# Experts placed by rank: double, full, half and quarter tiles in the two mixture-of-experts stages of a two-layer hybrid block

## The chip, the cores and the metric

The kernel runs on one core of a Trainium2 chip. The metric is the device time of one execution in microseconds (us). Three runs of the kernel before took 1410.01, 1413.93 and 2414.91 us; the median, 1413.93, is the time before.

## What is computed

Two layers act on 256 latent tokens and 256 context tokens of width 1024, all in float32. Layer 0 mixes with a gated delta rule and an S5 scan, layer 1 with latent attention (for the latent tokens alone). Each layer ends in a grouped top-2 mixture of 16 experts, and this is the part that the change touches:

```python
def grouped_moe(h, router_w, router_bias, w_gate, w_up, w_down):
    tok = h.reshape(-1, h.shape[-1])
    scores = jax.nn.sigmoid((tok @ router_w).astype(F32))
    ...
    _, idx = lax.top_k(jnp.where(in_group, choice, -jnp.inf), TOP_K)
    ...
    gates = jnp.sum(jax.nn.one_hot(idx, N_EXPERTS, dtype=F32) * wts[..., None], axis=1)
    out = jnp.zeros(tok.shape, F32)
    for e in range(N_EXPERTS):
        act = jax.nn.silu(tok @ w_gate[e]) * (tok @ w_up[e])
        out = out + gates[:, e:e + 1] * (act @ w_down[e])
```

`in_group` keeps the best of four groups of four experts. Layer 0 sends 512 tokens through its experts, layer 1 only the 256 latent ones, so 1024 and 512 rows in all, two for each token. An expert has a gate and an up matrix of 1024 x 512 and a down matrix of 512 x 1024, 2 MB each, and every layer has its own 16 experts. How many rows an expert gets is known only when the router has run.

## The kernel before

The program is straight-line code for five engines: TensorE (PE in the profile), VectorE (DVE, `V` in the code), ScalarE (ACT, `S`), GpSimd (POOL, `G`) and SyncE (SP), whose queue issues the weight loads. Each engine works off its own instructions one after the other, and waits at one until its operands are ready and its buffers free. The code names the engine of each instruction; the order on each engine is fixed when the kernel is built, by the framework's scheduler. It mostly follows the code, but lets some instructions overtake others (a Silu stands ahead of the result of a down product that the code issues before it), so the order has to be read from the built kernel.

**Placing.** `moe_route` counts the rows of each expert (`num`) and gives every row a tile of 128 rows and a place in it. Rows over an expert's cap go to extra tiles behind the `nst` fixed ones (`ovn`, `ovs`), which `overflow_loop` works off in a loop with as many turns as there are such tiles, up to `NOV`. In layer 0 every expert has one tile (cap 128); the expert with the most rows, if it has over 128, gets two and changes places with expert 8 (`BIGP`), so there are 17 tiles. The numbers of the experts are compile-time constants but for those that may have changed places: their number is read from the table `exi` into a register of SP by `expert_id` (the TENSOR_LOAD of line 1595), and the load's address is worked out from it. In layer 1 the tiles are 8, each with two experts of 64 rows each, in the order of their numbers.

**Weights.** `load_chunk` (line 199) issues the load of half a matrix, 1.05 MB, into one slot of a ring: nine slots in layer 0, 18 in layer 1. An expert is six chunks: gate (`wg`) 0 and 1, up (`wu`) 0 and 1, down (`wd`) 0 and 1.

**Layer 0, `experts0`.** TensorE multiplies here in a rounded float32 format, and gets full precision from three products. `wsplit` makes the high part of a chunk on ScalarE (`hi`, line 1660) and the low part on VectorE (`lo`, line 1661); for the first up chunk alone the low part is made on GpSimd. There are three pairs of such buffers (`HI`). `mm3` multiplies high by high, high by low and low by high: 24 products of 128 x 128 by 128 x 512 for a chunk, 72 for a tile. The rows of a tile come by an indirect DMA on GpSimd (`gather`), are turned on TensorE by `turn` (line 203) in groups of four, and split by `split` (`sp`, lines 1640 and 1641); the gated activations are turned and split in the same way. `gated` is the Silu on ScalarE and a product on VectorE. `write` scales the result of the down matrix on ScalarE (`y`, line 1730) and writes it out by an indirect DMA. The loop over units weaves two experts: gate of unit i, first gate chunk of unit i+1, turning of unit i's activations, second gate chunk of i+1, rows of i+2, down of i, both up chunks of i+1.

**Layer 1, `experts1`.** Products are full float32 here, with no split: each shows as two records on TensorE. Two experts of a tile write the two halves of 64 rows of the same result, so a chunk of each takes part in the same step. The rows of a tile are picked by a product with a one-hot table (`pick`, `sl` on VectorE), the results added back by a product with the gates (`put_back`). The loop weaves in the same way.

Of the kernel before, what the change touches and what calls it, by code (L numbers as in the profile page):

```python
# [31 lines left out]
NOV = 7  # L32
# [4 lines left out]
BIGP = 8  # L37
# [123 lines left out]
def _build(es, tc, I, O):  # L161
# [1136 lines left out]
    def moe_open(l, stack):  # L1298
# [41 lines left out]
        if l == 0:  # L1340
            m.xes = [m.mo.tile([128, D], F32, name=f"xe{i}") for i in range(3)]
            for t in m.xes:
                G.memset(t, 0.0)
            m.io16 = m.mo.tile([128, 16], F32, name="io16")
            m.far = m.mo.tile([128, 16], F32, name="far")
            G.tensor_copy(m.io16, sm[:, SM_IO16:SM_IO16 + 16])
            G.tensor_scalar(m.far[:, 0:BIGP], m.io16[:, 0:BIGP], 16.0 - BIGP, None, op0=OP.add)
            G.tensor_scalar(m.far[:, BIGP:16], m.io16[:, BIGP:16], float(BIGP), None, op0=OP.subtract)
            G.memset(m.far[:, 0:2], -1.0)
        else:  # L1350
            m.h2 = [m.mo.tile([128, D], F32, name=nm("h2k")) for _ in range(2)]
        return m
# [31 lines left out]
    def moe_route(m):  # L1384
        l, n, mo = m.l, m.n, m.mo
        cap = CAP0 if l == 0 else CAP1
        nst = 17 if l == 0 else 8
# [67 lines left out]
        t16, ovn, ovs, dif = rt([128, 16]), rt([128, 16]), rt([128, 16]), rt([128, 16])  # L1455
        if l == 0:


            key, kmx, big, ep = rt([128, 16]), rt([128, 1]), rt([128, 16]), rt([128, 16])
            V.scalar_tensor_tensor(key, num, float(cap), m.far, op0=OP.is_gt, op1=OP.mult)  # L1460
            red(kmx, key, OP.max)
            V.tensor_scalar(big, m.far, kmx, None, op0=OP.is_equal)
            V.tensor_scalar(key[:, 0:1], kmx, 16.0 - BIGP, -16.0, op0=OP.is_ge, op1=OP.mult)
            V.scalar_tensor_tensor(m.io16[:, BIGP:BIGP + 1], kmx, float(BIGP), key[:, 0:1], op0=OP.add, op1=OP.add)
            V.scalar_tensor_tensor(key, m.io16, float(BIGP), big, op0=OP.subtract, op1=OP.mult)
            tt(ep, m.io16, key, OP.subtract)
            m.exi = rt([128, 16], I32, True)
            V.tensor_copy(m.exi, ep)
            first, caps = rt([128, 16]), rt([128, 16])
            V.scalar_tensor_tensor(first, ep, float(BIGP), ep, op0=OP.is_gt, op1=OP.add)  # L1470
            V.tensor_scalar(caps, big, 128.0, 128.0, op0=OP.mult, op1=OP.add)
            V.scalar_tensor_tensor(num, big, -128.0, num, op0=OP.mult, op1=OP.add)
        V.tensor_scalar(ovn, num, float(cap), None, op0=OP.is_gt)
        for j in range(1, 3 if l == 0 else 2):
            V.scalar_tensor_tensor(ovn, num, float(cap + 128 * j), ovn, op0=OP.is_gt, op1=OP.add)
# [4 lines left out]
        if l == 0:  # L1480
            V.tensor_scalar(t16, t16, 128.0, 128.0 * nst, op0=OP.mult, op1=OP.add)
            tt(t16, t16, caps, OP.subtract)
            V.scalar_tensor_tensor(dif, first, 128.0, t16, op0=OP.mult, op1=OP.subtract)
            tt(val, rank, bc(caps[:, None], N16), OP.is_lt)
        else:
            V.tensor_scalar(t16, t16, 128.0, float(128 * nst - cap), op0=OP.mult, op1=OP.add)
            V.scalar_tensor_tensor(dif, sm[:, SM_IO16:SM_IO16 + 16], float(cap), t16, op0=OP.mult, op1=OP.subtract)
            V.tensor_scalar(val, rank, float(cap), None, op0=OP.is_lt)
# [10 lines left out]
        V.scalar_tensor_tensor(rin, tid, -128.0, rin, op0=OP.mult, op1=OP.add)  # L1499

# [83 lines left out]
    def overflow_loop(m, w2, body):  # L1584

        nreg = nc.values_load(m.novi[0:1, 0:1], min_val=0, max_val=NOV,
                              skip_runtime_bounds_check_because="at most 7 tiles can overflow")
# [24 lines left out]
    def experts0(m):  # L1612
        with ExitStack() as st:
# [19 lines left out]
            def split(name, p, n):  # L1633
# [10 lines left out]
                return hi, lo  # L1644

# [54 lines left out]
            def half(u, name, hh, parts=None):  # L1700

                wh, wl = parts or wsplit(gate_up_chunk(0, name, u[0].e, hh), G if (name, hh) == ("wu", 0) else V)
                for j in u:
                    if hh == 0:
                        setattr(j, name, ps(("wg", "wu").index(name)))
# [10 lines left out]
            def down(u):  # L1716
                for nh in range(2):
                    wh, wl = wsplit(down_chunk(0, u[0].e, nh), V)
# [15 lines left out]
            xe, jobs, eids = {}, {}, {0: 0, 1: 1}  # L1734
            order = [[t] for t in range(BIGP)] + [[BIGP, BIGP + 1]] + [[t] for t in range(BIGP + 2, m.nst)]

            def fetch(upto):
                while len(xe) + len(jobs) <= min(upto, m.nst - 1):
                    ti = len(xe) + len(jobs)
                    xe[ti] = gather(m.toki[:, ti:ti + 1])  # L1740

            def job(ti, u):
                if ti not in jobs:
                    if u not in eids:
                        eids[u] = expert_id(m.exi[0:1, u:u + 1])
                    j = jobs[ti] = Job()
                    j.e, j.ti = eids[u], ti
                    j.xT = split("x", turn(xe.pop(ti)), 8)
                return jobs[ti]

            def unit(i):
                return [job(ti, i) for ti in order[i]]
# [438 lines left out]
```

## Time and profile before

| | us |
|---|---|
| median of three runs | 1413.93 |
| the profiled execution | 1414.94 |
| its span in the profile | 1412.7 |
| first layer up to its experts (0 to 605) | 605 |
| first layer's experts (605 to 941.3) | 336.3 |
| second layer up to its experts (941.3 to 1155) | 213.7 |
| second layer's experts (1155 to 1402.5) | 247.5 |
| the end (1402.5 to 1412.7) | 10.2 |

In the first layer's experts TensorE is busy 322.44 of 336.3 us, VectorE 231.54, ScalarE 233.44, GpSimd 130.21, and the DMA engines move 310 GB/s; in the second layer's TensorE is busy 241.86 of 247.5, VectorE 47.53, ScalarE 20.39, GpSimd not at all, and the DMA engines move 337 GB/s. The clock that TensorE was granted is 0.942 of full speed over the span, 0.98 and 0.99 in the two stages.

A row of a group in the profile gives line, engine, operation and tiles (result <- operands), then busy time, the mean of one in ns, and the idle time of the engine just before them with what ended it. A row of one instruction begins with its start and its duration in us; consecutive alike ones are drawn together with their count. In a stretch of time each engine stands with its busy us and its instructions.

### The profile page before, as it was taken

To read this page: it belongs to the slowest core of one execution; us is meant where nothing else is said; L and a number is where in the kernel's file an instruction comes from. 1 tells how busy PE (TensorE), PEld (TensorE's weight loads), DVE (VectorE), ACT (ScalarE), POOL (GpSimd) and SP (SyncE) were. 2 spreads that over 40 slices of the span, in tenths; PEclk is the share of its full clock that TensorE was granted. 3 is DMA by queue.
4 is the path that set the end of the run, shared out by engine and by line. 5 is a ranking of instruction groups with operands and counts; after the bars stand their busy time and mean duration, and the time that the engine had idled before them with its cause. 6 is when DMAs were issued, how large, how long until landed. Compare 5 with 4: busy or idle time off the path is not lost. (4 is left out here: it accounts for less than half of the span.)

```text
span 1412.7 us, 18172 instructions
## 1 busy us (share of the span) xinstructions
PE 1251.5 (89%) x6716; PEld 847.8 (60%) x6716; DVE 787.6 (56%) x1460; ACT 529.6 (37%) x775; POOL 381.0 (27%) x266
## 2 busy tenths in 40 slices
PE   5889989899788999589999999976999669999996
PEld 1786655555327988457777777744777544444422
DVE  5776756844974465767775577775566151221112
ACT  3312634544112242167776477724365011000100
POOL 1443434320126330334443233353231020000000
PEclk9999999899798999789999999998999779999998
DMA  8713457767488345679999699753034569999980
GB/s 306 257 34 88 155 171 221 225 216 235 149 251 281 131 172 180 273 244 345 377 369 330 227 317 358 283 210 113 32 135 155 194 254 385 398 401 400 399 336 31
DMA packets 201805, 340.40 MB, mean 241 GB/s; under 512 B 31726, under 2 KB 70638, under 8 KB 201201
## 3 DMA queue, kind: packets, MB, share of 16 engines
q1 hardware_dynamic: 171952, 310.97, 62.3%
q10 hardware_dynamic: 23920, 16.95, 3.9%
q0 software_dynamic: 5840, 11.28, 2.2%
q8 instruction: 55, 0.90, 0.3%
q14 instruction: 38, 0.30, 0.1%
HBM read 320.56 MB, written 27.82 MB: 247 GB/s over the span
## 5 line engine op out<-in xcount | busy, mean ns | idle before, releaser
L206 PE MATMUL ps<-hi,sp 128*128 128x512 f32 x816 | 269.5, 404 | 6.0 <-ACT sp L1640 3.7
L1661 DVE TENSOR_TENSOR lo<-ch,hi 128x2048 fp32r<-128x2048 f32 x80 | 185.1, 2330 | 84.6 <-ACT hi L1660 79.8
L1660 ACT ACTIVATE hi<-ch 128x2048 fp32r<-128x2048 f32 x96 | 184.1, 1920 | 80.3 <-PE ps L206 52.8
L206 PEld LDWEIGHTS ps<-hi,sp 128*128 128x128 f32 x816 | 154.0, 190 | 42.7 <-ACT sp L1640 4.4
L206 PE MATMUL ps<-lo,sp 128*128 128x512 f32 x408 | 164.9, 404 | 3.2 <-DVE lo L1661 2.4
L206 PE MATMUL ps<-ch,stat 128*32 128x512 f32 x384 | 93.9, 646 | 31.7 <-DMA ch<-in_ada_w 30.6
L206 PE MATMUL ps<-ch,xT 128*64 128x512 f32 x480 | 119.7, 596 | 0.0
L1661 POOL TENSOR_TENSOR lo<-ch,hi 128x2048 fp32r<-128x2048 f32 x16 | 73.9, 4621 | 160.6 <-ACT hi L1660 160.6
L206 PEld LDWEIGHTS ps<-lo,sp 128*128 128x128 f32 x408 | 77.8, 191 | 26.9 <-DVE lo L1661 8.8
L206 PEld LDWEIGHTS ps<-ch,xT 128*64 128x64 f32 x480 | 36.1, 137 | 66.5 <-issue 65.2
L228 POOL TENSOR_TENSOR frs<-rs,sm 128x1 f32<-128x1 f32 x2 | 1.1, 560 | 259.8 <-DVE rs L227 259.8
L1867 ACT ACTIVATE aT<-ps 128x512 f32<-128x512 f32 x8 | 4.8, 597 | 149.1 <-PE ps L203 149.1
L206 PE MATMUL ps<-ch,aT 128*64 128x512 f32 x240 | 60.0, 596 | 0.7 <-ACTq L1588 0.7
L1880 DVE TENSOR_TENSOR y<-ps,bcm 128x512 f32<-128x512 f32 x16 | 11.1, 691 | 81.8 <-PE ps L206 81.8
L603 POOL TENSOR_TENSOR wl<-raw,wh 128x1024 fp32r<-128x1024 f32 x16 | 38.7, 2417 | 66.2 <-ACT wh L602 66.0
L206 PE MATMUL ps<-hH,wh 128*128 128x512 f32 x128 | 55.0, 430 | 0.0
L206 PEld LDWEIGHTS ps<-ch,stat 128*32 128x32 f32 x384 | 13.6, 112 | 67.7 <-DMA ch<-in_ada_w 35.0
L206 PE MATMUL ps<-hL,wh 128*128 128x512 f32 x128 | 53.8, 420 | 0.0
L206 PE MATMUL ps<-hH,wl 128*128 128x512 f32 x128 | 53.1, 415 | 0.0
L742 DVE SCALAR_TENSOR_TENSOR ac<-ps,convw,ac 128x510 f32<-128x510 f32 (+1 forms) x48 | 35.5, 740 | 23.7 <-ACT ac L738 23.3
L1152 POOL TENSOR_TENSOR ch<-ch,ch 128x512 fp32r<-128x512 f32 (+1 forms) x28 | 31.1, 1127 | 58.3 <-ACT ch L1151 32.3
L206 PE MATMUL ps<-y,sT 128*128 128x512 f32 x80 | 40.9, 642 | 6.4 <-DVE y L1880 2.3
(543 smaller groups left out, 2559.7 us busy)
## 6 DMA issues: line engine op xcount, KB each, us to landing
ch<-in_wg SPq DMA_DIRECT2D x63, 1024.0 KB
ch<-in_wd SPq DMA_DIRECT2D x62, 1024.0 KB
ch<-in_wu SPq DMA_DIRECT2D x61, 1024.0 KB
ch<-in_ada_w SPq DMA_DIRECT2D x88, 512.0 KB
raw<-in_w_in SPq DMA_DIRECT2D x16, 512.0 KB
bcm<-modd ACTq DMA_DIRECT2D x12, 512.0 KB
x<-in_xs SPq DMA_DIRECT2D x8, 512.0 KB
yd<-x SPq DMA_DIRECT2D x8, 512.0 KB
```

Source lines behind the costliest of these rows:

```text
L206: return T.matmul(out, l, r, start=start, stop=stop)
L228: G.tensor_tensor(out, t, bc(neghalf, [128, n]), op=OP.pow)
L603: eng.tensor_tensor(wl, w, wh.bitcast(F32), op=OP.subtract)
L742: V.scalar_tensor_tensor(ac[:, :, lo:hi], pv[:, :, lo + o:hi + o], convw[:, blk, j:j + 1], ac[:, :, lo:hi], op0=OP.mult, op1=OP.add)
L1152: eng.tensor_tensor(lo, src, hi.bitcast(F32), op=OP.subtract)
L1660: last_split[:] = (S.activation(hi, w, AF.Copy), eng.tensor_tensor(lo, w, hi.bitcast(F32), op=OP.subtract))
L1661: eng.tensor_tensor(lo, w, hi.bitcast(F32), op=OP.subtract))
L1867: S.activation(j.aT.rearrange("p k n -> p (k n)"), p, AF.Copy)
L1880: V.tensor_tensor(j.y[:, nh], p, g2[:, nh * 512:(nh + 1) * 512], op=OP.mult)
```

## The change

**Placing.** The router now ranks the experts by their rows. `key` is 16 times the count, with the expert's number taken off to break ties (`tie`); the first `STATIC` experts, 2 in layer 0 and 4 in layer 1, get a constant added, so that they keep the first places whatever their counts. `pos` is an expert's place, and the table `exi` now holds the expert of each place. Places 0 to `STATIC` - 1 are compile-time constants; the others are read into a register when their first chunk is loaded (`experts_of`).

In layer 0, place 2 (the most rows of the others) gets a double tile of 256 rows, places 3 to 9 a full tile of 128 each, and places 0, 1 and 10 to 15 half a tile of 64 each: 13 tiles, 0 (places 0, 1), 1 and 2 (place 2), 3 to 9 and 10 to 12 (places 10 to 15). In layer 1, places 0 to 11 get 64 rows each, two to a tile, and places 12 to 15 get 32 each in one tile: 7 tiles. Rows beyond these go to overflow tiles as before, up to 8 of them.

**Layer 0, half tiles.** A tile with two experts is worked in the form of layer 1: `pair` multiplies the loaded chunks unsplit in full float32, expert by expert in column groups of 64, and `whole` copies the turned rows without a split. Full and double tiles are worked as before. The order of the units is written out: tile 0, tile 10, the double, tile 11, places 3, 4, 5, tile 12, places 6, 7, 8, 9. The first gate chunk's split ahead of the first unit, and the ordering of the first rows behind it, are gone.

**Layer 1.** The order of the tiles is 0, 1, 2, 3, 6 (the quarters), 4, 5.

The diff, cut to what the prediction speaks of:

```diff
-NOV = 7
+NOV = 8
-BIGP = 8
+STATIC = (2, 4)
...
+        V.scalar_tensor_tensor(key, num, 16.0, m.tie, op0=OP.mult, op1=OP.add)
+        tt(cmp, bc(key[:, None, :], SQ), bc(key[:, :, None], SQ), OP.is_gt)
+        red(pos[:, :, None], cmp, OP.add)
         if l == 0:
-            key, kmx, big, ep = rt([128, 16]), rt([128, 1]), rt([128, 16]), rt([128, 16])
...
+            V.tensor_scalar(first, pos, 10.0, 64.0, op0=OP.min, op1=OP.mult)
+            V.scalar_tensor_tensor(first, pos, 2.5, first, op0=OP.is_gt, op1=OP.mult)
+            V.scalar_tensor_tensor(first, pos, 64.0, first, op0=OP.mult, op1=OP.add)
...
+        tt(oh, bc(sm[:, SM_IO16:SM_IO16 + 16, None], SQ), bc(pos[:, None, :], SQ), OP.is_equal)
+        tt(oh, oh, bc(sm[:, None, SM_IO16:SM_IO16 + 16], SQ), OP.mult)
+        red(key[:, :, None], oh, OP.add)
+        m.exi = rt([128, 16], I32, True)
+        V.tensor_copy(m.exi, key)
...
+    def experts_of(m):
+        ids = {p: p for p in range(STATIC[m.l])}
+        def get(p):
+            if p not in ids:
+                ids[p] = expert_id(m.exi[0:1, p:p + 1])
+            return ids[p]
+        return get
...
+            def whole(name, p, n):
+                o = w2.tile([128, n, 128], F32R, tag=f"{name}h", name=nm("wh")).bitcast(F32)
+                for i in range(n // 4):
+                    S.activation(o[:, 4 * i:4 * i + 4], p(i).rearrange("p (k n) -> p k n", k=4), AF.Copy)
+                return o
...
+            def pair(p, xT, k0, ws, n):
+                for q in range(4):
+                    for b, w in enumerate(ws):
+                        c = slice(64 * b, 64 * b + 64)
+                        mm(p[c], xT[:, k0 + q, c], w[:, q, :], k0 + q == 0, k0 + q == n - 1)
...
+                if len(u[0].es) == 2:
+                    pair(getattr(u[0], name), u[0].xT, 4 * hh, [gate_up_chunk(0, name, e(), hh) for e in u[0].es], KD)
+                    return
+                wh, wl = wsplit(gate_up_chunk(0, name, u[0].es[0](), hh), G if (name, hh) == ("wu", 0) else V)
...
-            order = [[t] for t in range(BIGP)] + [[BIGP, BIGP + 1]] + [[t] for t in range(BIGP + 2, m.nst)]
+            one = {p: ([p], [p]) for p in range(3, 10)}
+            order = [([0], [0, 1]), ([10], [10, 11]), ([1, 2], [2]), ([11], [12, 13]), one[3], one[4], one[5],
+                     ([12], [14, 15]), one[6], one[7], one[8], one[9]]
...
-            for i in range(16):
+            for i in range(len(order)):
...
-                    if i < 14 and len(nxt) == 1:
-                        job(order[i + 2][0], i + 2)
+                    if i + 2 < len(order) and len(nxt) == 1:
+                        job(order[i + 2][0][0], order[i + 2][1])
...
-                return job([2 * ti, 2 * ti + 1], lambda kk, i: m.ohT[:, kk, i, c], m.tokf[:, c], m.gate[:, c])
+                return job([lambda p=p: who(p) for p in ((2 * ti, 2 * ti + 1) if ti < 6 else range(12, 16))],
+                           lambda kk, i: m.ohT[:, kk, i, c], m.tokf[:, c], m.gate[:, c])
```

How the change moves instructions is seen in the order of each engine's rows, at three places. The first is ScalarE in layer 0, between two experts with a full tile each. `hi` is the high part of a chunk, `sp` of turned rows or activations, `act` the Silu, `y` the scaled result. Before, `hi_5847` is that of the next expert's first up chunk, whose low part GpSimd makes:

```order
L1660 ACTIVATE hi_5824<-ch_5822 128x2048
L1640 ACTIVATE sp_5755<-ps_5757 128x512
L1660 ACTIVATE hi_5847<-ch_5845 128x2048
L1640 ACTIVATE sp_5785<-ps_5787 128x512
L1713 ACTIVATE act_5882<-ps_5742 128x512
L1640 ACTIVATE sp_5785<-ps_5794 128x512
L1730 ACTIVATE y_5801<-ps_5808,rt_4949 128x512
L1660 ACTIVATE hi_5866<-ch_5864 128x2048
```

After the change the same copy is `hi_5844`:

```order
L1654 ACTIVATE sp_5754<-ps_5756 128x512
L1681 ACTIVATE hi_5820<-ch_5818 128x2048
L1654 ACTIVATE sp_5781<-ps_5783 128x512
L1654 ACTIVATE sp_5781<-ps_5790 128x512
L1745 ACTIVATE act_5878<-ps_5732 128x512
L1681 ACTIVATE hi_5844<-ch_5842 128x2048
L1767 ACTIVATE y_5797<-ps_5804,rt_4949 128x512
```

The high part of the first up chunk has moved from ahead of the turned rows (`sp_5785`, now `sp_5781`) and the Silu to behind them.

The second place is ScalarE after a half-tile pair, where a single expert (place 3) follows; `wh` is the pair's turned activations, `y` its two results, `bcm` a load that ScalarE issues, and `hi_5688` the high part of place 3's first up chunk:

```order
L1664 ACTIVATE wh_5612<-ps_5613 128x512
L1745 ACTIVATE act_5722<-ps_5590 128x512
L1654 ACTIVATE sp_5637<-ps_5639 128x512
L1654 ACTIVATE sp_5637<-ps_5646 128x512
L1211 DMA bcm_5725<-modd 128x1024
L1211 DMA bcm_5727<-modd 128x1024
L1767 ACTIVATE y_5653<-ps_5654,rt_4949 128x512
L1767 ACTIVATE y_5653<-ps_5668,rt_4949 128x512
L1681 ACTIVATE hi_5688<-ch_5686 128x2048
```

On TensorE there the pair's last down product stands directly ahead of the first product that reads `hi_5688`:

```order
L206 MATMUL ps_5668<-ch_5671,wh_5612 64x512
L206 MATMUL ps_5685<-hi_5688,sp_5467 128x512
L206 MATMUL ps_5685<-lo_5689,sp_5467 128x512
```

Such a pair has no counterpart before, where every expert's down matrix was split; what has moved is that a high part now stands behind the results of the down matrix (`y`) and so behind the products that make them.

The third place is the queue of SP in layer 1, behind its first 20 loads. Before it is loads alone; `ISA` below is arithmetic on a register:

```order
L199 DMA x<-in_wu 128x4x512
L199 DMA ch_9654<-in_wu 128x4x512
L199 DMA ch_9680<-in_wg 128x4x512
L199 DMA ch_9682<-in_wg 128x4x512
L199 DMA ch_9699<-in_wg 128x4x512
L199 DMA ch_9701<-in_wg 128x4x512
```

After the change:

```order
L199 DMA x<-in_wu 128x4x512
L199 DMA ch_8915<-in_wu 128x4x512
L1609 TENSOR_LOAD rt_8629
L199 ISA
L199 DMA ch_8944<-in_wg 128x4x512
L1609 TENSOR_LOAD rt_8629
L199 ISA
L199 DMA ch_8949<-in_wg 128x4x512
```

From the third tile on, an expert's number is read from the table before its first load is issued.

More of the change, by code (lines that the diff above doesn't have):

```diff
@@ L1385, in moe_route @@
         l, n, mo = m.l, m.n, m.mo
-        cap = CAP0 if l == 0 else CAP1
-        nst = 17 if l == 0 else 8
+        nst = 13 if l == 0 else 7
         ntl = nst + NOV
@@ L1473, in moe_route @@
-        V.tensor_scalar(ovn, num, float(cap), None, op0=OP.is_gt)
-        for j in range(1, 3 if l == 0 else 2):
-            V.scalar_tensor_tensor(ovn, num, float(cap + 128 * j), ovn, op0=OP.is_gt, op1=OP.add)
+        key, pos, first, caps = (rt([128, 16]) for _ in range(4))
+        cmp, oh = (t[:, i:i + 256].rearrange("p (a b) -> p a b", a=16) for i in (0, 256))
+        SQ = [128, 16, 16]
+        V.scalar_tensor_tensor(key, num, 16.0, m.tie, op0=OP.mult, op1=OP.add)
+        tt(cmp, bc(key[:, None, :], SQ), bc(key[:, :, None], SQ), OP.is_gt)
@@ L1476, in moe_route @@
+        tt(num, num, caps, OP.subtract)
+        V.tensor_scalar(ovn, num, 0.0, None, op0=OP.is_gt)
+        for j in range(1, 4 if l == 0 else 2):
+            V.scalar_tensor_tensor(ovn, num, float(128 * j), ovn, op0=OP.is_gt, op1=OP.add)
         V.tensor_tensor_scan(ovs, ones[:, 0:16], ovn, 0.0, op0=OP.mult, op1=OP.add)
@@ L1479, in moe_route @@
         rank = kp[:, 0:16 * n].rearrange("p (t e) -> p t e", e=16)
[L1480 to L1488, printed above, removed]
+        V.tensor_scalar(t16, t16, 128.0, 128.0 * nst, op0=OP.mult, op1=OP.add)
+        tt(t16, t16, caps, OP.subtract)
+        tt(dif, first, t16, OP.subtract)
+        tt(val, rank, bc(caps[:, None], N16), OP.is_lt)
         tt(val, val, bc(dif[:, None], N16), OP.mult)
@@ L1586, in overflow_loop @@
         nreg = nc.values_load(m.novi[0:1, 0:1], min_val=0, max_val=NOV,
-                              skip_runtime_bounds_check_because="at most 7 tiles can overflow")
+                              skip_runtime_bounds_check_because="at most 8 tiles can overflow")
         with tc.For_i(0, nreg, 1) as it:
@@ L1733, in write, with job @@
                                              out_offset=bass.IndirectOffsetOnAxis(ap=m.rowi[:, cs], axis=0))
[L1734 to L1735 removed]
+            xe, jobs, who = {}, {}, experts_of(m)
+            one = {p: ([p], [p]) for p in range(3, 10)}
+            order = [([0], [0, 1]), ([10], [10, 11]), ([1, 2], [2]), ([11], [12, 13]), one[3], one[4], one[5],
+                     ([12], [14, 15]), one[6], one[7], one[8], one[9]]
+            tiles = [ti for ts, _ in order for ti in ts]
             def fetch(upto):
                 while len(xe) + len(jobs) <= min(upto, m.nst - 1):
[L1739 removed]
+                    ti = tiles[len(xe) + len(jobs)]
                     xe[ti] = gather(m.toki[:, ti:ti + 1])
[L1742 removed]
+            def job(ti, places):
                 if ti not in jobs:
[L1744 to L1745 removed]
                     j = jobs[ti] = Job()
[L1747 to L1748 removed]
+                    j.es, j.ti = [lambda p=p: who(p) for p in places], ti
+                    j.xT = (whole if len(places) == 2 else split)("x", turn(xe.pop(ti)), 8)
                 return jobs[ti]
             def unit(i):
[L1752 to L1753 removed]
+                return [job(ti, order[i][1]) for ti in order[i][0]]
             fetch(1)
[L1755 to L1757 removed]
+            unit(0)
+            unit(1)
             fetch(2)
@@ L1760, in experts0 @@
                 for hh in range(2):
-                    half(unit(0), name, hh, first if (name, hh) == ("wg", 0) else None)
-            for i in range(16):
+                    half(unit(0), name, hh)
+            for i in range(len(order)):
                 cur = unit(i)
@@ L1769, in experts0 @@
                             g2[c] = bc_mod(w1, 0, c, 5, f"g2{c}")
-                fetch(order[i][-1] + 3)
-                nxt = unit(i + 1) if i < 15 else None
+                fetch(tiles.index(order[i][0][-1]) + 3)
+                nxt = unit(i + 1) if i + 1 < len(order) else None
                 if nxt:
@@ L1774, in experts0 @@
                 for j in cur:
-                    j.aT = split("a", turn(j.a), 4)
+                    j.aT = (whole if len(j.es) == 2 else split)("a", turn(j.a), 4)
                 if nxt:
                     half(nxt, "wg", 1)
-                    if i < 14 and len(nxt) == 1:
-                        job(order[i + 2][0], i + 2)
+                    if i + 2 < len(order) and len(nxt) == 1:
+                        job(order[i + 2][0][0], order[i + 2][1])
                     write(cur)
```

65 lines of the change are left out of this document (31 added, 34 removed).

## The prediction

> **What bounds the kernel now.** I read the page first, then stretches of time by engine, then each stage's rows. The profiled execution took 1414.94 us, 1.0 us above the median 1413.93; the sum below is made against 1414.94. Runs of this kernel differ by a few microseconds, so changes within 2% (28 us) count as none.
>
> ```profile
> span 1412.7 us, 18172 instructions
> ...
> 600.00:620.00 20.00, 15.39 (x80) 8.97 (x79) 10.66 (x14) 7.97 (x8) 11.22 (x6) 0.76 0.69 235
> 680.00:700.00 20.00, 19.90 (x91) 15.72 (x90) 15.13 (x10) 15.91 (x13) 8.22 (x4) 1.00 1.04 371
> 1200.00:1220.00 20.00, 20.00 (x100) 9.12 (x98) 4.80 (x10) 2.39 (x4) 0.00 (x0) 1.00 1.05 400
> ```
>
> The columns after the stretch are PE, PEld, DVE, ACT, POOL (busy us, instructions), granted clock, DMA share, GB/s. Both expert stages keep TensorE full and the DMA engines almost so. Which of the two sets the pace has to come from each stage.
>
> First layer, TensorE's rows, from the first transposition to the last weight product:
>
> ```profile
> 604.95 0.65 PE L203 MATMUL ps<-cm,xe 128*128 128x128 f32 x4
> ...
> 907.38 0.63 PE L206 MATMUL ps<-hi,sp 128*128 128x512 f32 x2
> ...
> 911.58 0.63 PE L206 MATMUL ps<-hi,sp 128*128 128x512 f32 x2
> ...
> 914.38 0.40 PE L206 MATMUL ps<-hi,sp 128*128 128x512 f32 x1
> 914.62 0.60 PE L203 MATMUL ps<-cm,act 128*128 128x128 f32 x4
> 914.97 0.48 PE L206 MATMUL ps<-hi,sp 128*128 128x512 f32 x1
> ...
> 940.91 0.40 PE L206 MATMUL ps<-hi,sp 128*128 128x512 f32 x1
> ...
> SPq L199 <- DVE lo L1661: 31.6, 16, 2.6
> 690.56 4.64 POOL L1661 TENSOR_TENSOR lo<-ch,hi 128x2048 fp32r<-128x2048 f32 x1 [10.27 <-ACT hi L1660]
> 709.22 4.61 POOL L1661 TENSOR_TENSOR lo<-ch,hi 128x2048 fp32r<-128x2048 f32 x1 [10.26 <-ACT hi L1660]
> ```
>
> 907.38 to 911.58 holds 18 products, 0.233 us each. A group of four transpositions costs 0.45 with its change-over (0.36 until the next product starts at 914.97, 0.1 in that product). A full tile is 72 products and three groups: 18.15 us. One expert follows the other in 18.66 (690.56 to 709.22), so **the first layer's experts wait for TensorE**. The queue that loads weights waits for buffers to be split (the SPq row, 640 to 700). The stage lasts 604.95 to 941.31 = 336.4 us: 17 tiles are 308.6, waits and slow starts 27.8.
>
> Second layer:
>
> ```profile
> 1155.01 5.73 PE L206 MATMUL ps<-sl,h2k 128*128 128x128 f32 x32 [1.79 <-DVE sl L1824]
> ...
> 1182.49 3.65 PE L206 MATMUL ps<-ch,xT 128*64 128x512 f32 x16
> ...
> 1196.76 3.60 PE L206 MATMUL ps<-ch,xT 128*64 128x512 f32 x16
> ...
> 1225.80 7.04 PE L206 MATMUL ps<-ch,xT 128*64 128x512 f32 x32
> ...
> 1396.10 3.65 PE L206 MATMUL ps<-ch,aT 128*64 128x512 f32 x14
> 1400.53 1.98 PE L206 MATMUL ps<-y,sT 128*128 128x512 f32 x4 [0.79 <-DVE y L1880]
> ...
> 1365.00:1370.00 5.00, 5.00 (x26) 1.72 (x24) 0.00 (x0) 0.60 (x1) 0.00 (x0) 1.00 1.05 408
> 1370.00:1375.00 5.00, 4.22 (x18) 1.21 (x16) 1.38 (x2) 0.00 (x0) 0.00 (x0) 1.00 0.35 129
> ```
>
> An expert pair takes 29.04 us on TensorE (1196.76 to 1225.80, the same place in two tiles); eight last 1155.01 to 1402.51 = 247.5. A half matrix for two experts, 16 records (a full-precision product is two), costs 3.63. The weights end at 1371.6 (129 GB/s x 5 us = 0.65 MB, 1.6 us at 408 GB/s), though TensorE uses the last only at 1396.10. So TensorE bounds here too, **with the loads only 24.5 us behind it**.
>
> **The change part by part.** The router's counts, computed from the reference with its inputs, are 36 55 46 43 99 80 71 52 72 47 27 58 132 51 78 77 in the first layer and 23 44 31 6 47 60 50 17 34 11 42 45 17 19 27 39 in the second. Placed as the change does, the largest in each class are 132 of 256, 99 of 128, 55 of 64; then 60 of 64 and 19 of 32. Nothing overflows in either layer.
>
> *First layer, work.* Nine full tiles stay: 9 x 18.15 = 163.4. Eight experts go to four half-tile pairs, in the form of the second layer's rows: six halves x 3.63 + 3 x 0.45 = 23.1 each, 92.5 for four. Together 255.9 against 308.6: **-52.7 us**. The low parts that vanish (48 of 96 splits) stood beside TensorE, and give nothing by themselves.
>
> *First layer, waits.* The waits of splits turn on these rows:
>
> ```profile
> 707.21 1.92 ACT L1660 ACTIVATE hi<-ch 128x2048 fp32r<-128x2048 f32 x1 [0.82 <-PE ps L206]
> ...
> L1661 POOL TENSOR_TENSOR lo<-ch,hi 128x2048 fp32r<-128x2048 f32 x16 | 73.9, 4621 | 160.6 <-ACT hi L1660 160.6
> L1640 ACT ACTIVATE sp<-ps 128x512 fp32r<-128x512 f32 x51 | 29.1, 586 | 10.4 <-PE ps L203 10.2 <-ACT hi L1660 0.2
> L1730 ACT ACTIVATE y<-ps,rt 128x512 f32<-128x512 f32 x32 | 22.0, 687 | 23.8 <-PE ps L206 23.8
> ...
> 707.01 0.60 PE L203 MATMUL ps<-cm,xe 128*128 128x128 f32 x4
> ...
> 714.62 0.39 PE L206 MATMUL ps<-lo,sp 128*128 128x512 f32 x1
> ```
>
> The first half of an up matrix has its low part made on POOL (4.62 us). Let T be when the gate is done. Before, the high part starts at T+0.2 (707.21), the low part is ready at 713.83, and TensorE wants it at 714.62: 0.8 us to spare. In the changed order of ScalarE that high part stands behind two `sp` copies and the Silu. The second copy's transpositions follow a first down product, so the Silu ends near T+2.7. The low part is ready at T+2.7+1.92+0.1+4.62 = T+9.3, wanted at T+7.6 by the row, or T+6.8 by pure work: a wait of 1.7 to 2.5. I take 2.2 for five such experts: 11 us. Behind the waiting product stands all of TensorE.
>
> After a half-tile pair it is worse: the high part stands behind the pair's second `y` copy, which ends 0.7 after its last product. TensorE waits 0.1+0.69+1.92+0.1 = 2.8 for the high part, then 4.8 for POOL's low part, less one product: 7.6, twice (places 3 and 6). I laid the changed rows of all engines behind one another with these durations; the order of before, laid out likewise, gives 334 where the trace has 336.4. It shows further waits: 3.6 at the double expert's up matrix, 5.0 and 2.8 around place 5, 4.2 at hand-overs and the end, 2 in shorter ones. Sum 11+15.2+3.6+7.8+4.2+2 = 44.
>
> A wait also slows what follows:
>
> ```profile
> 792.88 0.73 PE L206 MATMUL ps<-hi,sp 128*128 128x512 f32 x2 [1.71 <-DVE sp L1641]
> ...
> 780.00:800.00 20.00, 16.68 (x73) 13.07 (x72) 9.33 (x8) 7.69 (x7) 1.02 (x1) 0.91 0.75 260
> 792.00:796.00 4.00, 3.12 (x9) 2.50 (x10) 1.42 (x3) 0.00 (x0) 0.00 (x0) 0.73 0.68 238
> ```
>
> After waits of 1.6 and 1.7 us the clock falls to 0.73 for about four microseconds; the 20 us lose 9%, 1.8 us. The changed order has four long waits and five near 2.2; I charge six such dips, 10 us. So the stage takes 255.9+44+10 = 309.9 against 336.4: **-26.5 us**. Half of the work saved comes back as waits on splits.
>
> The Trainium skill ("TensorE: Matmul & The Clock Gate", Part 1) says that about 3.4 us of idleness drops the array to half rate until it has been busy as long. By that rule only the four long waits would count: 4 x 1.7 = 7 us instead of 10. The trace agrees in kind: 0.73 in a stretch that is partly at half rate, though two waits either side of a few products were enough.
>
> *First layer, loads.* 88 of 96 chunks of 1.05 MB come during the stage; at the 400 GB/s of the last window above that is 231 us, with 8.4 MB of gathered and scattered rows 252, below 310. Pairs ask faster (12 chunks need 31.5 us, a pair 23.1), but nine buffers and the double expert (37 us of work on six chunks) cover that.
>
> *Second layer.* One tile fewer is -29.0. The four-expert tile issues 32 records for a half. The nearest row of that form:
>
> ```profile
> 600.17 4.85 PE L206 MATMUL ps<-ch,stat 128*32 128x512 f32 x32
> ...
> 600.00:604.00 4.00, 4.00 (x36) 0.67 0.62 196
> ...
> L206 PE MATMUL ps<-ch,stat 128*32 128x512 f32 x384 | 93.9, 646 | 31.7 <-DMA ch<-in_ada_w 30.6 <-DMA perm<-in_c_perm 0.8
> ```
>
> 4.85 us at a clock of about 0.67 is 3.3 at full clock, as four at once would give; the whole group's mean, 0.245 a record, would be 7.8. Between 3.63 and 7.8 a half I take the first, nearest to the row with its clock known, plus 2.5 for products that stand alone between 128-wide ones; the upper end would add 25. TensorE would then be done at 1155+247.5-29.0+2.5 = 1376. The loads, however, keep their bytes: the last lands at 1371.6 and needs the tail of before, 1402.51-1396.10 = 6.4, so 1378.0. The loads take over as the bound, -24.5; with two chains so close I leave 2.5 for their waits on each other: **-22 us**.
>
> Twelve experts there are now found through a register:
>
> ```profile
> L1595 SPq TENSOR_LOAD <-rt x14: 265/274/472, 608.8 to 879.4; - x14
> L199 SPq FUSED_REGOPS  x84: 42/46/51, 609.3 to 900.8; - x84
> L199 SPq MOVE ch<-in_wg x28: 29/29/29, 609.5 to 882.3; - x28
> ...
> 1351.68 8.85 SPq L199 DMA_DIRECT2D ch<-in_wd  x4
> ```
>
> 12 x 0.27 + 72 x 0.075 = 8.7 us of SP's queue, spread over 72 issues that already take over 2 us each (8.85 for four): covered while the DMA queue is full. If each instead delayed its load, the cost is 8.7; if such loads run only at the 371 GB/s of the first layer's stretch above, 72 x (2.83-2.57) = 19. I take 0, since the first layer's rate is set by its TensorE.
>
> *Routing.* The path to the tables gains four 256-wide operations and a few 16-wide:
>
> ```profile
> L1433 DVE TENSOR_TENSOR cmp<-rt 128x256 f32<-128x256 f32 x1 | 0.4, 418 | 0.0
> L1397 DVE TENSOR_TENSOR rt<-rt,rt 128x16 f32<-128x16 f32 x4 | 0.7, 169 | 0.0
> ```
>
> First layer: 4 x 0.4 less what it replaces, +1.5. Second layer: 4 x 0.4 and some ten small ones that start 0.1 apart, +2.5. TensorE has nothing else there, so both count: **+4 us**.
>
> **Sum:** 1414.94 - 26.5 - 22 + 4 = **1370 us**.
>
> **The rivals.**
> *The waits stay away.* If the split queues kept their slack, the first layer would be 255.9+27.8: -52.7, and 1414.94-52.7-22+4 = **1344**. For it: before has these waits nearly at nothing. Against: the order of rows.
> *The second layer gains almost nothing*, because register-found loads stream at 371 GB/s: +19, **1389**. For it: the first layer's stretch shows no more. Against: its DMA was not the bound.
> *The placing overflows* and a loop of extra tiles runs, so the change doesn't do what it says. One tile costs about 18.7 and six unhidden loads of 2.6, 34 us: **1404**. Against: the counts.
> *Slower: the clock.* If the many waits of the first layer keep the granted clock low on average, 255.9 us of work costs 255.9/c. From c = 0.82 on (56 us, more than the gain of 45 and the 10 already charged) nothing is left. At 0.76, as in 600 to 620, it is 81 instead of 10: **1441**. Against: a 20 us stretch with a sixth of it idle has 0.91, and the new stage is idle for a seventh. A steady 0.91 would be 25 instead of 10, 1385. The Trainium skill's rule of half rate after 3.4 us of idleness would do this only if such idleness came in nearly every window.
>
> **How the numbers follow.** Forecast 1370, from 1355 to 1386: 0.60. No waits, 1344: 0.13; between it and the forecast 0.05. Second layer without most of its gain, 1389: 0.13. Overflow 0.03. Clock, 1441: 0.06. The range 1342 to 1395 leaves out the last two and the edges. Faster by over 2% (under 1385.7) takes the first three, 0.78; within 2%, 0.16; slower 0.06.
>
> **What would show it.** 648 split products in place of 1224, and 384 records of the 64-wide form in that stage; waits of TensorE on POOL's low part, near 2 us at five experts and over 4 at two; no overflow loop; a first expert stage near 310 us. In the second layer a stage near 222 us with DMA at 400 GB/s until TensorE's last down product. The prediction is wrong if those waits are missing, if the last stage still ends 20 us or more behind its loads, or if the clock of the first stage lies under 0.9.

## The result: 2.5% faster, and half of the first layer's expected gain missing

The changed kernel takes 1377.09 us (median of four, 1374.01 to 1380.24) against 1412.68 for the kernel before: a ratio of 0.975, with an interval of 0.972 to 0.979. (The median before is of four runs, one of them the disturbed one of 2414.91 us, which the ratio leaves out.) The profiled execution took 1380.24. The forecast was 1370.

Of the kernel after, the two expert stages, from the first transposition or pick to the last weight product (the second to its last product); the columns are those of the first view in the prediction:

```profile
span 1378.5 us, 17491 instructions
...
601.19:923.68 322.49, 281.01 (x1192) 171.34 (x1188) 135.81 (x85) 133.92 (x125) 76.46 (x32) 0.94 0.87 318
923.68:1141.28 217.60, 170.41 (x794) 126.33 (x794) 123.77 (x350) 73.88 (x178) 56.99 (x52) 0.88 0.45 161
1141.28:1367.86 226.58, 220.84 (x1076) 87.85 (x1076) 41.37 (x79) 18.00 (x29) 0.00 (x0) 0.99 0.95 363
```

The same two stages before:

```profile
604.95:941.31 336.36, 322.49 (x1432) 252.16 (x1428) 231.55 (x153) 233.49 (x196) 130.27 (x49) 0.98 0.87 310
1155.01:1402.51 247.50, 241.87 (x1120) 98.99 (x1120) 47.52 (x91) 20.39 (x33) 0.00 (x0) 0.99 0.89 337
```

The first stage became 13.9 us shorter where 26.5 were forecast, the second 20.9 (22 forecast). The stretch between grew by 3.9 (213.7 to 217.6), the stretch ahead of the first stage is 3.8 shorter, the end 0.5 longer: together 34.2, the difference of the spans. The stretch ahead is not put down to the change: its code is the same but for the ranking, and in the profiles of this study the first stage begins anywhere from 599.1 to 614.0. Single executions differ by that much, so **stages are compared below, not only totals**. A stage varies too: four profiles hold the changed kernel's first expert stage as it is (the one above, and those of the three experiments on the second layer), and it takes 318.2, 318.5, 319.5 and 322.5 us in them. The one above is the longest of the four.

What TensorE waited for in the first stage after (total, times, longest):

```profile
PE ps L206 <- POOL lo L1682: 21.6, 8, 4.1
PE ps L206 <- ACT hi L1681: 8.0, 4, 2.6
PE ps L206 <- DMA ch<-in_wu: 4.0, 2, 3.5
PE ps L206 <- DVE lo L1682: 3.7, 4, 1.8
PE ps L203 <- DVE act L1746: 1.6, 2, 0.8
PE ps L203 <- DVE sp L1655: 1.6, 1, 1.6
PE ps L206 <- ACT sp L1654: 0.7, 1, 0.7
```

That is 41 us where the prediction had 44, and the places are those it named, but for the 4.0 us of waits for loads, of which it had none. The single waits on TensorE's rows (start, duration, work, and in brackets the wait ahead):

```profile
679.09 0.80 PE L206 MATMUL ps<-lo,sp 128*128 128x512 f32 x1 [3.12 <-POOL lo L1682]
...
735.53 0.50 PE L206 MATMUL ps<-hi,sp 128*128 128x512 f32 x1 [2.61 <-ACT hi L1681]
740.13 0.80 PE L206 MATMUL ps<-lo,sp 128*128 128x512 f32 x1 [4.11 <-POOL lo L1682]
...
762.23 0.50 PE L206 MATMUL ps<-lo,sp 128*128 128x512 f32 x1 [2.28 <-POOL lo L1682]
...
782.82 0.50 PE L206 MATMUL ps<-lo,sp 128*128 128x512 f32 x1 [2.28 <-POOL lo L1682]
...
870.13 0.50 PE L206 MATMUL ps<-lo,sp 128*128 128x512 f32 x1 [2.30 <-POOL lo L1682]
...
890.73 0.50 PE L206 MATMUL ps<-lo,sp 128*128 128x512 f32 x1 [2.28 <-POOL lo L1682]
...
909.55 0.50 PE L206 MATMUL ps<-lo,sp 128*128 128x512 f32 x1 [1.36 <-POOL lo L1682]
```

2.3 at single experts, 1.4 at the last (forecast 2.2), 2.6 + 4.1 = 6.7 behind a pair (7.6), 3.1 at the double (3.6). The product at 762.23 has the chain ahead of it on record: the high part, on ScalarE right behind the Silu, then the low part on GpSimd, which ends at 762.17.

```profile
755.12 0.59 ACT L1745 ACTIVATE act<-ps 128x512 f32<-128x512 f32 x1
755.59 1.92 ACT L1681 ACTIVATE hi<-ch 128x2048 fp32r<-128x2048 f32 x1
757.59 4.58 POOL L1682 TENSOR_TENSOR lo<-ch,hi 128x2048 fp32r<-128x2048 f32 x1 [1.46 <-ACT hi L1681]
```

Before, that row on ScalarE (at 707.21, in the prediction's rows) stands ahead of the Silu, and TensorE waits for GpSimd's low part once in the whole stage (the Silu's row, and the wait's total, times, longest):

```profile
709.51 0.59 ACT L1713 ACTIVATE act<-ps 128x512 f32<-128x512 f32 x1
...
PE ps L206 <- POOL lo L1661: 0.7, 1, 0.7
```

### The profile page after: what moved, and what is told of

The parts are those of the page before. It is cut to its first block, busy times and chain, and to the rows that moved or that the text cites. A ratio compares the mean times of both kernels' runs of the same rounds, so it can differ in the third digit from the quotient of the medians.

```text
span 1378.5 us, 17491 instructions
## 1 busy us (share of the span) xinstructions
PE 1181.7 (86%) x6432; PEld 751.9 (55%) x6432; DVE 691.9 (50%) x1398; ACT 423.9 (31%) x699; POOL 326.5 (24%) x250
## 5 line engine op out<-in xcount | busy, mean ns | idle before, releaser
L206 PE MATMUL ps<-hi,sp 128*128 128x512 f32 x432 | 147.1, 416 | 8.8 <-ACT hi L1681 8.0
L1682 DVE TENSOR_TENSOR lo<-ch,hi 128x2048 fp32r<-128x2048 f32 x40 | 108.4, 2736 | 76.7 <-ACT hi L1681 76.7
L206 PE MATMUL ps<-lo,sp 128*128 128x512 f32 x216 | 90.8, 420 | 25.4 <-POOL lo L1682 21.6
L206 PE MATMUL ps<-ch,xT 128*64 128x512 f32 (+1 forms) x488 | 109.7, 596 | 0.4 <-DMA ch<-in_wg 0.2
L206 PEld LDWEIGHTS ps<-hi,sp 128*128 128x128 f32 x432 | 85.2, 199 | 32.3 <-ACT hi L1681 11.7
L206 PE MATMUL ps<-ch,wh 128*64 128x512 f32 x384 | 96.6, 614 | 4.0 <-DMA ch<-in_wu 4.0
L1681 ACT ACTIVATE hi<-ch 128x2048 fp32r<-128x2048 f32 x48 | 91.1, 1915 | 26.7 <-issue 22.2
L206 PEld LDWEIGHTS ps<-lo,sp 128*128 128x128 f32 x216 | 42.8, 198 | 42.0 <-POOL lo L1682 25.0
L206 PE MATMUL ps<-ch,aT 128*64 128x512 f32 (+1 forms) x232 | 53.3, 597 | 2.1 <-DMA ch<-in_wd 1.4
L1682 POOL TENSOR_TENSOR lo<-ch,hi 128x2048 fp32r<-128x2048 f32 x8 | 36.5, 4557 | 63.4 <-ACT hi L1681 63.4
## 6 DMA issues: line engine op xcount, KB each, us to landing
ch<-in_wu SPq DMA_DIRECT2D x62, 1024.0 KB, 12.6
```

Source lines behind the costliest of these rows:

```text
L206: return T.matmul(out, l, r, start=start, stop=stop)
L1681: last_split[:] = (S.activation(hi, w, AF.Copy), eng.tensor_tensor(lo, w, hi.bitcast(F32), op=OP.subtract))
L1682: eng.tensor_tensor(lo, w, hi.bitcast(F32), op=OP.subtract))
```

## The experiments

### The slow low part

```diff
-                wh, wl = wsplit(gate_up_chunk(0, name, u[0].es[0](), hh), G if (name, hh) == ("wu", 0) else V)
+                wh, wl = wsplit(gate_up_chunk(0, name, u[0].es[0](), hh), V)
```

> The changed kernel, with the low part of the first up chunk made on VectorE like all others, not on GpSimd. Theory (TensorE waits for the slow low part, 4.6 us on GpSimd against 2.3 on VectorE): the five waits of 1.4 to 2.3 us at single experts vanish, the one at the double expert falls from 3.1 to about 0.8, the two behind half-tile pairs from 4.1 and 3.9 to about 1.8: 17 us, and 2 to 4 us of half clock behind them. First expert stage about 303 us where it was 322.5, time about 1357. Rival (VectorE becomes the late one, since it then makes all 48 low parts): the waits stay and are put down to VectorE, stage 316 or more, time 1370 or more.

Measured: 1357.64 us, ratio to the kernel before 0.961 (0.955 to 0.967), 19.5 us below the changed kernel. The stage is 299.5 us (604.73 to 904.24), 23.0 less than in the changed kernel's profile and 18.7 to 23.0 less than in the four. TensorE's waits in it:

```profile
PE ps L206 <- ACT hi L1681: 8.0, 4, 2.6
PE ps L206 <- DVE lo L1682: 7.9, 7, 1.8
PE ps L206 <- DMA ch<-in_wu: 4.5, 2, 3.5
```

21.6 + 3.7 us for low parts became 7.9, so 17.4 us of waits are gone, as expected, and VectorE did not become late. The rest of the 23 is clock: what it takes of TensorE's busy time (worked out as further below) fell from 13.8 to 8.1. That part is uncertain: two of the other profiles of the same stage have 9.5 and 12.2 where this one has 13.8.

VectorE got eight low parts more, and yet is busy in the stage for 136.6 us where it was 135.8, since its low parts had taken longer while GpSimd was at its own. In the changed kernel one takes 2.29 us on VectorE alone, and 4.38 where it overlaps one on GpSimd:

```profile
773.56 2.29 DVE L1682 TENSOR_TENSOR lo<-ch,hi 128x2048 fp32r<-128x2048 f32 x1
...
778.21 4.55 POOL L1682 TENSOR_TENSOR lo<-ch,hi 128x2048 fp32r<-128x2048 f32 x1 [1.45 <-ACT hi L1681]
...
780.54 4.38 DVE L1682 TENSOR_TENSOR lo<-ch,hi 128x2048 fp32r<-128x2048 f32 x1 [4.69 <-ACT hi L1681]
```

In that profile the 32 low parts on VectorE that overlap none on GpSimd take 2.28 to 2.30 us, the eight that do 3.9 to 4.9; with this edit all 48 take 2.28 to 2.30.

The same edit on the kernel **before**, where the line reads nearly the same:

> The kernel before (not the changed one), with the low part of the first up chunk made on VectorE. Theory (the slow low part costs time only where the high part ahead of it comes late, which is so in the changed order and not in the order of before): no change, time within 5 us of before, 1413, and the first expert stage within 4 us of 336.4. Rival (the low part on GpSimd costs its time in any order): the stage falls by 15 us or more, as it did in the changed kernel.

Measured: 1411.78, ratio 0.998 (0.995 to 1.001); stage 335.7. No change. GpSimd's 4.6 us cost nothing while the high part stood ahead of the turned rows and the Silu; behind them they cost 2.3 us an expert. It is the order that the change brought which made them late: this rests on the rows above and on these two runs, since no run moves the high part back in the changed kernel.

### The two pairs at the start

```diff
-            order = [([0], [0, 1]), ([10], [10, 11]), ([1, 2], [2]), ([11], [12, 13]), one[3], one[4], one[5],
+            order = [([0], [0, 1]), ([1, 2], [2]), ([10], [10, 11]), ([11], [12, 13]), one[3], one[4], one[5],
```

(the rows of three tiles are fetched at the start, not of two)

> The changed kernel, with the double expert second in the order of units (pair, double, pair, pair, then as it is), so that two pairs no longer start the stage. Theory (24 chunks asked for by two pairs in 46 us outrun the loads): TensorE's waits for loads of the up matrix near the start (0.5 and 3.5 us), the half clock behind them (about 3 us) and the waits that follow at the hand-over go: 7 to 9 us, time about 1369. Rival (the loads fall behind wherever pairs stand close together): the waits come back at the two pairs behind the double, time within 3 us of the changed kernel's.

Measured: 1371.32, ratio 0.970 (0.965 to 0.975); stage 312.1 (601.55 to 913.66), 6.1 to 10.4 less than in the four profiles, the total 5.8 less: near the 7 to 9 that the theory expected. The waits for loads near the start are gone (0.6 in all where they were 4.0). But place 3, now behind two pairs in a row, waits 3.4 us for a high part instead of 2.6, and the rival is partly right: in the combined kernel below, which keeps this order, ScalarE's row for that high part names a load:

```profile
729.77 1.91 ACT L1681 ACTIVATE hi<-ch 128x2048 fp32r<-128x2048 f32 x1 [8.09 <-DMA ch<-in_wu]
```

### Products that stand alone

TensorE's rows of the changed kernel where a pair follows place 5; the 128*64 rows of two records are one product of one expert, torn from its half by the scheduler:

```profile
786.96 1.47 PE L206 MATMUL ps<-ch,wh 128*64 128x512 f32 x2
...
795.38 1.07 PE L206 MATMUL ps<-ch,wh 128*64 128x512 f32 x2
796.38 1.03 PE L203 MATMUL ps<-cm,xe 128*128 128x128 f32 x7
797.34 3.65 PE L206 MATMUL ps<-ch,wh 128*64 128x512 f32 x14
```

At full clock the lone product takes 1.0 us (795.38 to 796.38), and the 14 records left still take the 3.6 us of a whole half: its partner runs alone too.

```diff
-                        mm(p[c], xT[:, k0 + q, c], w[:, q, :], k0 + q == 0, k0 + q == n - 1)
+                        with ExitStack() as st2:
+                            if last_pe:
+                                st2.enter_context(tc.issue_after(last_pe[0].ins))
+                            last_pe[:] = [mm(p[c], xT[:, k0 + q, c], w[:, q, :], k0 + q == 0, k0 + q == n - 1)]
```

> The changed kernel, with the products of a half-tile pair in the first layer tied behind the product issued before them in the code, so that none of them can stand alone between split products. Theory (a product of one column group alone costs 1.0 us where it costs 0.45 beside its neighbour, and seven halves are torn like this): 3 to 5 us less in the first expert stage, waits as they are, time about 1373. Rival (the lone products fill time in which TensorE waits anyway): the waits beside them grow by as much, no change.

Measured: 1374.32, ratio 0.973 (0.968 to 0.978), overlapping the changed kernel's interval; the total does not tell it from no change. The stage is 314.5 where the four profiles have 318.2 to 322.5. TensorE's busy time, less what the clock took of it, is 263.9 us against 267.3: **3.4 us of work** less, as expected. Its waits are 41.2 us where they were 41.5, so the rival, by which they grow, falls.

### The second layer's tiles, registers and order

The placing of before (16 fixed places, eight tiles) in the second layer alone:

```diff
-STATIC = (2, 4)
+STATIC = (2, 16)
-        nst = 13 if l == 0 else 7
+        nst = 13 if l == 0 else 8
-            order = [0, 1, 2, 3, 6, 4, 5]
+            order = list(range(8))
```

(`first` is 64 times the place, `caps` 64 everywhere)

> The changed kernel, with the second layer's experts placed as before: all 16 in fixed places, eight tiles of two experts with 64 rows each, in their order, no number read from a table. The router's new ranking stays. Theory (the second layer's gain is one tile less, partly eaten by products that stand alone): its stage is back at about 247 us where it was 226.6, the first layer's at 322 as in the changed kernel, time about 1398. Rival (the gain in the second layer comes from a better placed start of its loads, not from the tiles): its stage stays under 240, time under 1390.

Measured: 1398.04, ratio 0.989 (0.983 to 0.994); second stage 246.6, first 318.2. The second layer's 20 us are the tile, with the order of the tiles, which this edit puts back too; the registers, which it takes out as well, are tested next.

Constants in place of the numbers from the table:

```diff
-        ids = {p: p for p in range(STATIC[m.l])}
+        ids = {p: p for p in range(STATIC[0])} if m.l == 0 else dict(enumerate([0, 1, 2, 3, 5, 6, 4, 11, 10, 15, 8, 14, 13, 7, 12, 9]))
```

> The changed kernel, with the second layer's experts by place written in as constants (the places that the router finds for these inputs), so that no load there is addressed through a register. The ranking itself still runs. Theory (SyncE's register work stands beside a full queue): no change, time within 4 us of 1377, loads at 400 GB/s as before. Rival (loads found through a register stream more slowly or start later): the second expert stage falls by 8 to 19 us.

Measured: 1377.71, ratio 0.975 (0.970 to 0.981); stage 226.9 with 362 GB/s where it was 226.6 with 363. The registers cost nothing.

Every product of `experts1` (`mmc`, in place of `mm`) tied behind the one issued before it:

```diff
+            def mmc(*a):
+                with ExitStack() as st2:
+                    if last:
+                        st2.enter_context(tc.issue_after(last[0].ins))
+                    last[:] = [mm(*a)]
```

> The changed kernel, with all products of the second layer's experts tied to the order in which the code issues them, so that the scheduler can't put single ones between products of another shape. Theory (a full-precision product that stands alone costs 1.0 us where two column groups together cost 0.45; some 20 of them cost the 7.7 us by which the stage misses the gain of a whole tile): stage about 220 us where it was 226.6, time about 1370. Rival 1 (the loads bound the stage: they ended 214 us behind its start, and the tail of before was 6.4 us): no more than a few us, with TensorE waiting for loads in the last 40 us. Rival 2 (the free order hides waits for VectorE): TensorE waits for VectorE at the picks or at the adding back, stage no shorter.

Measured: 1379.06, ratio 0.977 (0.971 to 0.983); stage 227.9. No gain, though TensorE is busy 5.1 us less (215.7 for 220.8). Its waits in the stage say why:

```profile
PE ps L206 <- DMA ch<-in_wu: 5.4, 4, 1.6
PE ps L206 <- DMA ch<-in_wd: 4.7, 4, 1.5
PE ps L206 <- DVE sl L1867: 1.8, 1, 1.8
PE ps L206 <- SPq L1592: 1.4, 1, 1.4
```

The time of the lone products turned into waits for loads, 10.1 us where the changed kernel has 1.6. They stream at 400 GB/s in the middle of the stage:

```profile
1250.00:1300.00 50.00, 47.13 (x303) 19.04 (x292) 5.94 (x10) 4.78 (x8) 0.00 (x0) 1.00 1.05 400
1300.00:1340.00 40.00, 34.39 (x140) 10.25 (x138) 5.21 (x9) 1.19 (x2) 0.00 (x0) 1.00 1.05 400
```

Rival 1 holds: the loads end 217 us behind the stage's start, here as in the changed kernel and in the kernel before (not 214 as the expectation has it: 216.6 follows from the prediction's rows). With one tile less, **loads and TensorE bound this stage within a few microseconds of each other**.

### Causes together

The low part on VectorE, the double second, and the results of pairs on VectorE:

```diff
+                    yh = j.y[:, nh * 512:(nh + 1) * 512]
+                    if len(u[0].es) == 2:
+                        V.tensor_scalar(yh, p, m.gate[:, cs], None, op0=OP.mult)
+                    else:
+                        S.activation(yh, p, AF.Copy, scale=m.gate[:, cs])
```

> Three edits on the changed kernel together: the first up chunk's low part on VectorE, the double expert second in the order, and the results of half-tile pairs scaled and copied by VectorE, so that the high part behind a pair no longer stands behind them on ScalarE. Theory (the three causes add): 20 us by the first, 6 by the second, and 5 by the third (the waits of 2.6 and 1.7 behind pairs become one of about 3.0, twice, and half clock behind them gets shorter): time about 1346. Rival (the waits have one cause in common, ScalarE as a whole, and only move): no more than 5 us below the 1357.6 of the first edit alone.

Measured: 1353.24, ratio 0.958 (0.953 to 0.963). That is 4.4 below the first edit, where the theory had 11 and the rival no more than 5: by the total the rival's number came. The stage is 292.5, 7.0 below the first edit's. Behind the pair in front of place 6 there is one wait of 2.6, as expected; behind the two pairs in front of place 3 the load quoted above keeps 3.4 + 1.5. So that part of the theory failed on the order of units, and the rival's reason, ScalarE as a whole, is not what the rows show there.

```diff
+            order = [([0], [0, 1]), ([1, 2], [2]), ([10], [10, 11]), one[3], one[4], ([11], [12, 13]), one[5], one[6], ([12], [14, 15]), one[7], one[8], one[9]]
+                if nxt and len(cur[0].es) == 1 and len(nxt[0].es) == 2:
+                    dp = [wsplit(down_chunk(0, cur[0].es[0](), nh), V) for nh in range(2)]
```

(with the tied products; `down` uses `dp` where it is made)

> The combined kernel (low part on VectorE, results of pairs on VectorE) with three more edits: the pairs spread out (pair, double, pair, places 3, 4, pair, 5, 6, pair, 7, 8, 9), a pair's products tied behind the product issued before them, and, where a pair follows a single expert, that expert's down matrix split ahead of the pair's second gate half. Theory (the waits that are left in the combined kernel, 3.4 for loads behind two pairs in a row, 2.5 and 1.8 where a single expert is followed by a pair, and 3.4 us of lone products, each have the cause named): first expert stage about 280 us where the combined kernel has 292.5, time about 1341. Rival (three pairs of split buffers are too few for splits made earlier: the waits move to the next expert's up matrix): stage 288 or more, time 1349 or more.

Measured: 1345.67, ratio 0.951 (0.948 to 0.955); stage 284.5 (609.10 to 893.60), between the two expectations. TensorE waits for no weights in it; of 14.3 us of waits that are left most are for VectorE:

```profile
PE ps L206 <- DVE lo L1682: 8.1, 6, 2.6
PE ps L203 <- DVE act L1749: 3.3, 4, 0.9
```

> The kernel with the pairs spread out, but with the units in the order of the changed kernel (pair, pair, double, pair, 3, 4, 5, pair, 6 to 9); all other edits stay. Theory (two pairs at the start outrun the loads): 5 to 8 us longer in the first expert stage than with the pairs spread out, with waits for loads of the up matrix near 640 us. Rival (once the splits come early the order of units no longer matters): within 3 us of it.

Measured: 1346.58, ratio 0.952 (0.949 to 0.956); stage 287.6 (605.33 to 892.98), 3.1 longer, with the wait of 3.5 us for an up matrix at 649.22 back. Too little for the theory; the totals don't differ, and 3.1 us are less than the 4.3 by which the same stage varied above. So spreading the pairs removes that wait, but a gain in time is not shown. The results of pairs on VectorE, the tied products and the early splits together are worth about 12 us (299.5, the first edit's stage in the same order, to 287.6). This kernel and the one with the pairs spread out are the fastest here, 2.3% below the changed kernel (1345.67 of 1377.09).

## Why the prediction was right, and where it was off

**First layer.** The sum by its terms, against the profile of after. TensorE's busy time is split by the granted clock: in stretches of 2 us, busy time times what the clock lacks of 1 (before: 5.6 us of 322.5).

| term | forecast | measured |
|---|---|---|
| work at full clock | 255.9 | 281.0 - 13.8 = 267.3 |
| waits | 44 | 41.5 |
| slow clock | 10 | 13.8 |
| stage | 309.9 | 322.5 |

The waits on splits held, in size and place: the order of the rows, laid out with the durations of before, showed them, and the rival without waits fell. So did the counts (432 + 216 split products, 384 records of the 64-wide form). That the sum of the waits is so near is in part luck, since 4.0 of the 41.5 are the loads. The rival of the low clock was too dear (0.94, not 0.76).

**The step that failed is the work.** The prediction took 0.233 us for a split product from rows of nothing else, and called all that was left of the stage of before "waits": by the split used here, 316.9 us of its 336.4 were work, 8.3 more than the 308.6 it worked out. From each row's start to the next one's, without waits and with the slow clock taken off, a split product costs 0.242 us in the stage of before, and about as much after: the 648 products cost 156.5 us, where the prediction's 18 in 4.20 us make 151.2, so 5.3 more. The pairs' products cost 92.1 where 24 halves of 3.63 are 87.1: 5.0 more, of which 3.4 are lone products, by the experiment that tied them, and 1.6 stay open. The transpositions cost 18.4 where 39 groups of 0.45 are 17.6. Together this is 11.2 of the 11.4 us missing.

The slow clock has six spells in this profile, as many as the prediction charged, but of 2.3 us each, not 1.7; one of them stands behind a load. The loads were wrong at one place: "nine buffers and the double expert cover that" missed that two pairs come ahead of the double (4.0 us of waits, and half clock behind the longer one).

**Second layer.** -20.9 against -22. The form of the quarter tile was sized rightly: a half of it takes the 3.6 us of a half of a pair, with twice the records.

```profile
1252.13 3.64 PE L206 MATMUL ps<-ch,xT 128*32 128x512 f32 x32
```

But the lone products and the small waits around them were not 2.5 us: from the first turning of activations to the last the stage takes 185.10 us (1168.59 to 1353.69) where before took 206.43 (1181.91 to 1388.34); less one tile of 29.04 that is 7.7 more, 5.1 of it products, by the experiment that tied them. So TensorE's own sum failed by 5 us, and the total came out because the loads stood right behind, as the prediction had it: when the lone products went, the stage stayed. That it came out to 1.1 us is luck. The loads ended at 1358.3 (267 GB/s x 5 us = 1.3 MB, 3.3 us at 409), 9.6 us ahead of the stage's end where the prediction had 6.4 and set its test at 20:

```profile
1350.00:1355.00 5.00, 3.49 (x16) 1.12 (x12) 0.69 (x1) 0.56 (x1) 0.00 (x0) 1.00 1.05 409
1355.00:1360.00 5.00, 4.91 (x19) 1.63 (x20) 0.69 (x1) 0.04 (x1) 0.00 (x0) 1.00 0.71 267
```

**Routing.** The waits of TensorE for the tables were 6.40 and 4.61 us, and are 8.07 and 7.45 (first fence before, second after):

```profile
596.88 0.18 PE L206 MATMUL ps<-rt,rt 128*128 128x24 bf16 x1 [6.40 <-DVE rt L1397]
...
1152.42 0.81 PE L206 MATMUL ps<-rt,rt 128*128 128x15 bf16 x20 [4.61 <-DVE rt L1397]
```

```profile
592.11 0.18 PE L206 MATMUL ps<-rt,rt 128*128 128x21 bf16 x1 [8.07 <-DVE rt L1394]
...
1138.68 0.81 PE L206 MATMUL ps<-rt,rt 128*128 128x15 bf16 x20 [7.45 <-DVE rt L1394]
```

+1.7 and +2.8 make 4.5 (forecast 4). No overflow loop ran in either layer.

**The total.** Measured against forecast it is 7 us off (1377.09 for 1370), inside the stated range. Stage by stage the miss is larger: 12.6 us are missing in the first layer, and 3.8 came back in the stretch ahead of it, which is put down to chance.

## What to carry to other kernels

An instruction that costs nothing costs its full lateness once a new order puts it behind something else: ask of every slow helper by how much it is early now (0.8 us here), and read that again from the new order. Take the price of an instruction from its mean over a whole stage, not from its purest stretch (0.242 us here, not 0.233), and keep what lies between apart from waits. When one bound is lowered, look how far the next one lies behind: here it was 24.5 us, and a cleaner order of products could give nothing beyond it.

## What was not expected of the hardware

The clock behind a wait has two values, not shades. In the changed kernel behind the waits of 2.6 + 4.1 us and behind two of 2.3 us, those that end at 762.2 and at 782.8 (stretch, columns as above; the clock is third from the right):

```profile
740.00:743.00 3.00, 2.87 (x7) 2.31 (x8) 3.00 (x2) 0.00 (x0) 0.08 (x1) 0.50 1.05 393
...
764.00:766.00 2.00, 2.00 (x10) 1.63 (x9) 2.00 (x2) 0.86 (x1) 1.19 (x1) 1.00 0.97 349
...
785.00:787.00 2.00, 2.00 (x6) 1.06 (x5) 0.00 (x0) 0.00 (x0) 0.79 (x1) 0.50 1.04 389
```

It is half clock or full: cut into quarters of a microsecond, the first expert stage has 1133 stretches of 1.00, 145 of 0.50 and 13 between. The Trainium skill ("TensorE: Matmul & The Clock Gate", Part 1) says so, with about 3.4 us of idleness as the condition; by that rule the waits of 2.3 us should never do it. Mostly they don't: of 24 waits of 2.3 us at single experts (four each in six profiles in which GpSimd makes that low part) three were followed by half clock for some 3 us, the rest by 1.00, and the same wait is now one, now the other in kernels with the same first layer. Six waits of 3.1 us and more on GpSimd's part, in two profiles, were all followed by half clock, though one in each profile was shorter than 3.4 us. So the condition measured here is softer than the Trainium skill's.

The clock records say how. They change value only on a grid of 3.41 us, and every half-clock spell in the first expert stages lasts one, two or three steps of it. Over these stages in eleven profiles (all but that of the kernel before with its low part on VectorE), a step at full clock in which TensorE's rows leave 60% or more idle was followed by half clock 34 times of 34, one with 50% or less in none of 881, and between the two in 8 of 19. A step at half clock was followed by another where over 17% of it was idle (34 of 34), and by full clock where less was (39 of 39). A wait of 2.3 us is two thirds of a step, so what it does depends on how much of it falls into one step. (The ends of TensorE's products are modelled in the profile, so these shares are not exact.)
